# Gated linear unit: the tanh kept in its PSUM bank, two gates in one slot, the product taken for the hi and the lo part

## The chip, the cores and the metric

One core of one Trainium2 chip. Engines: TensorE (PE in the rows), VectorE (DVE), ScalarE (ACT), GpSimd (POOL) and SyncE (SP), which issues the DMAs. The metric is the device time of one execution in microseconds (us); the kernel before takes 1267.82 us, the median of three runs that lie between 1267.17 and 1268.06.

## The reference

A two-layer decoder trunk on x[1024, 1024] in float32. Each layer normalises x, projects it to queries, keys, values, an SSM input and three gates, runs three groups side by side, and projects their gated outputs back into the residual:

```python
h = _rms(x, norm_g[l])
z = h @ w_in[l]
aq, ak, av, ag, su, sg, xq, xg = split(z)
out_a = sliding_window_attn(aq, ak, av, sinks[l]) * silu(ag)
out_b = s5(su, ...) * silu(sg)
out_c = cross_attn(xq, mk, mv) * silu(xg)
x = x + concat([out_a, out_b, out_c]) @ w_out[l]
```

The edited code is the end of s5, the SSM group, which is 512 channels wide, together with the gate that follows it:

```python
y = gelu(y)
y = y * sigmoid(y @ w_glu + b_glu)
out_b = y * silu(sg)
```

With sigmoid(v) = (1 + tanh(v/2))/2 the output is (1 + tanh(v/2)) * y * silu(sg)/2. The halves are folded into weights and stored gates, so that the kernel computes (tanh + 1) * g * y.

## The kernel before, in words

Float32 matmuls are made of three passes over operands that are split into a hi and a lo part of a rounded format (names in h and l: yh and yl, wh and wl, gh and gl). Their sum is the float32 value, and a float32 tensor that feeds a matmul is split by a ScalarE cast (hi) and a GpSimd or VectorE subtraction (lo).

Every operation is recorded on a tape first. A list scheduler (`order`, line 210) then lays the whole tape out with a cost for each instruction (`price`, line 349), and `issue` (line 323) emits it; so each engine's instructions stand in an order that is fixed when the kernel is built, and all carry line 333 in the profile. Engines run their own order and wait for one another by semaphores. SBUF is cut into slots by a table (`PLAN`, line 59): a name may lie in the slots listed for it, and a slot's next tile waits for the last user of the one before. PSUM is dealt out by the scheduler itself, in eight banks, at most two of them at a time for tiles of kind kq (`CAP`, line 344); a tile takes the bank that has been free the longest and holds it until its last user is done.

The unit `glu` (line 1391) is woven with the cross-attention into the memory (names xq, xpr, xph, xpl, bg, xg) in `run`, at line 1568, and the scheduler fills TensorE from what comes next too: the output projection of the attention group (mm, gh, gl, o, mg) and, in layer 1 of the input, the last columns of the gate projections (fc, fg), which are stored to gscr in DRAM. For each of two halves of the sequence the unit loads y from yscr, splits it into yh and yl, and makes four blocks m of 128 channels. A block takes twelve matmuls of 128x512 into a kq tile, a gate g fetched from gscr by a DMA, the elementwise work, and `mixed_store` (line 784), which splits the result into the hi and lo tiles o of the output projection (a ScalarE cast and a GpSimd subtraction). There are 2 layers, 2 halves and 4 blocks: 16 gates in all.

The gate's SBUF home is `gt`, slot R0 alone (line 92), 128x1024 wide. Before, it holds one gate at a time: g in one half, the tanh in the other. So block m+1 can fetch its g only when the o of block m are made. The kq bank is read once, by the tanh.

Of the kernel before, what the change touches and what calls it, by code (L numbers as in the profile page):

```python
# [11 lines left out]
F32 = mybir.dt.float32  # L12
F32R = mybir.dt.float32r
I32 = mybir.dt.int32
AF = mybir.ActivationFunctionType
ALU = mybir.AluOpType
# [383 lines left out]
class Trunk:  # L400
# [990 lines left out]
    def glu(self, l):  # L1391
        nc, a = self.nc, self.a
        bg = self.t("bglu", [P, 4])
        b0 = self.t("yt", [P, 512])[0:4, 0:P]
        nc.sync.dma_start(b0, a["b_glu"][l].rearrange("(m p) -> m p", p=P))
        pb = self.bg1()
        nc.tensor.transpose(pb[:, 0:4], b0, self.ident[0:4, 0:4])
        nc.scalar.activation(bg, pb[:, 0:4], AF.Copy, scale=0.5)
        wv = a["w_glu"][l].rearrange("(k p) n -> p k n", p=P)
        ws = [self.wload([(None, wv[:, :, 256 * i : 256 * i + 256])], [P, 4, 256], 0.5, "m") for i in range(2)]  # L1400
        for half in range(2):
            yp = [[self.t(n, [P, 2, 512], F32R) for _ in range(2)] for n in ("yh", "yl")]
            yh, yl = ([z[m // 2][:, m % 2] for m in range(4)] for z in yp)
            for m in range(4):
                yt = self.t("yt", [P, 512])
                jh = slice(half * 64, half * 64 + 64)
                nc.sync.dma_start(yt.rearrange("p (s j) -> p s j", s=LC), self.ys[m][:, :, jh])

                ov = lambda z: z.rearrange("p (b s j) -> p b s j", b=4, s=LC)
                yv = yt.rearrange("p (s b j) -> p b s j", s=LC, b=4)  # L1410
                nc.scalar.copy(ov(yh[m]), yv)
                nc.gpsimd.tensor_tensor(ov(yl[m]), yv, ov(yh[m]).bitcast(F32), op=ALU.subtract)
                yield
            self.mixed(1, half)
            for m in range(4):
                wh, wl = ws[m // 2]
                c = slice(m % 2 * P, m % 2 * P + P)
                ps = self.mm1("kq")
                n = 0
                for k in range(4):  # L1420
                    for w, y in ((wh, yh), (wh, yl), (wl, yh)):
                        nc.tensor.matmul(ps, w[:, k, c], y[k], start=n == 0, stop=n == 11)
                        n += 1
                th, g = self.carve("gt", [512, 512])
                nc.sync.dma_start(g, self.gscr[1, half, m])
                nc.scalar.activation(th, ps, AF.Tanh, bias=bg[:, m : m + 1])
                nc.vector.scalar_tensor_tensor(th, th, 1.0, g, op0=ALU.add, op1=ALU.mult)
                nc.gpsimd.tensor_tensor(g, yh[m].bitcast(F32), yl[m].bitcast(F32), op=ALU.add)
                nc.vector.tensor_tensor(g, g, th, op=ALU.mult)
                self.mixed_store(1, half, m, g)  # L1430
                yield

# [181 lines left out]
```

## Time and profile before

| | us |
|---|---|
| median of three runs | 1267.82 |
| profiled execution | 1271.33 |
| its span in the trace | 1269.6 |
| TensorE busy | 1237.5 (97%) |
| VectorE busy | 843.1 (66%) |
| ScalarE busy | 544.9 (43%) |
| GpSimd busy | 363.7 (29%) |
| mean granted TensorE clock | 0.995 of full speed |

The trace is of one execution. An engine that is 97% busy leaves some 32 us of idle time; the rows below show where in the edited stretches that idle time lies, and what ended it: an arrow "<-DVE xg" behind an idle time says that VectorE's instruction writing xg was the last thing waited for. Idle time of the other engines costs nothing in itself.

### The profile page before, as it was taken

How to read it: one execution, taken by the hardware profiler on the slowest of the kernel's cores; microseconds unless marked ns; L12 is line 12 of the kernel's file. 1: busy time of each engine (PE TensorE's matmuls, PEld its weight loads, DVE VectorE, ACT ScalarE, POOL GpSimd, SP SyncE). 2: the span in 40 equal slices, each digit the busy share in tenths (PEclk: the TensorE clock that was granted, in tenths of full speed). 3: DMA queues.
4: the chain of work that ended last, by engine and by line, in shares of the span. 5: the costliest groups of instructions: out<-in, count | busy, mean ns of one | idle time of the engine just before them, and what ended most of it. 6: DMA issues, size and time to landing. Idle time of an engine off the chain costs nothing.

```text
span 1269.6 us, 20347 instructions
## 1 busy us (share of the span) xinstructions
PE 1237.5 (97%) x7179; PEld 1046.1 (82%) x7179; DVE 843.1 (66%) x1941; ACT 544.9 (43%) x1320; POOL 363.7 (29%) x585
## 2 busy tenths in 40 slices
PE   8999999999999999899999999999999999899998
PEld 6987888898887988688878787899797897668886
DVE  6879889747788678632477888865787675444311
ACT  5463323336566666310344223344656575442100
POOL 1371010154342366310082100044342211283100
PEclk9999999999999999999999999999999999999999
DMA  8254545511225765773554555441313542377532
GB/s 245 62 138 114 150 138 170 145 45 54 85 77 153 212 184 150 214 224 125 183 136 114 145 145 147 120 113 42 105 35 124 174 131 76 98 235 244 177 108 75
DMA packets 190456, 171.79 MB, mean 135 GB/s; under 512 B 59625, under 2 KB 142097, under 8 KB 190354
## 3 DMA queue, kind: packets, MB, share of 16 engines
q1 hardware_dynamic: 190354, 170.48, 46.0%
q8 instruction: 57, 0.93, 0.3%
q14 instruction: 45, 0.37, 0.1%
HBM read 114.81 MB, written 46.72 MB: 127 GB/s over the span
## 4 chain that ended last, share of the span: by engine, by line
PE 82%; DMA 7%; DVE 4%; ACT 3%; POOL 2%; issue 2%; SPq 1%; DVEq 0%; ACTq 0%; POOLq 0%
PE mm L333 27%; PE fc L333 23%; PE bg L333 17%; PE kq L333 13%; DMA so<-kscr 3%; PE tp L333 2%; POOL o L333 1%; DMA raw<-in_w_in 1%; DMA x<-xr 1%; DMA xt<-x 1%; DMA graw<-in_w_out 1%; DMA gt<-gscr 1%; DMA gscr<-fg 1%; DVE hl L333 1%; SPq L333 1%
## 5 line engine op out<-in xcount | busy, mean ns | idle before, releaser
L333 PE MATMUL fc<-hh,fh 128*128 128x512 f32 x512 | 205.2, 401 | 2.0 <-DVE fg L333 1.6
L333 PE MATMUL fc<-hl,fh 128*128 128x512 f32 x512 | 205.7, 402 | 0.0
L333 PE MATMUL fc<-hh,fl 128*128 128x512 f32 x512 | 204.2, 399 | 0.1
L333 PE MATMUL mm<-ph,o 128*128 128x512 f32 x512 | 161.4, 395 | 0.0
L333 PEld LDWEIGHTS fc<-hh,fh 128*128 128x128 f32 x512 | 96.4, 188 | 21.7 <-DVE fg L333 2.4
L333 PEld LDWEIGHTS mm<-ph,o 128*128 128x128 f32 x512 | 95.9, 188 | 21.7
L333 PEld LDWEIGHTS fc<-hh,fl 128*128 128x128 f32 x512 | 96.7, 189 | 19.5 <-issue 1.2
L333 PEld LDWEIGHTS fc<-hl,fh 128*128 128x128 f32 x512 | 96.7, 189 | 17.1
L333 PE MATMUL kq<-ml,hh 128*128 128x256 f32 x384 | 109.2, 285 | 0.0
L333 PE MATMUL kq<-mh,hh 128*128 128x256 f32 x384 | 108.7, 286 | 0.0
L333 PE MATMUL kq<-mh,hl 128*128 128x256 f32 x384 | 108.7, 284 | 0.0
L333 PE MATMUL mm<-pl,o 128*128 128x512 f32 x256 | 101.1, 395 | 0.0
L333 PE MATMUL mm<-gh,o 128*128 128x512 f32 x256 | 85.4, 402 | 7.3 <-ACT gh L333 3.6
L333 POOL COPY ifs<-f 128x16 f32<-128x16 f32 x64 | 18.8, 315 | 209.8 <-PE tp L333 209.0
L333 DVE TENSOR_TENSOR xr<-xr,mm 128x512 f32<-128x512 f32 x32 | 21.9, 685 | 85.6 <-PE mm L333 85.5
L333 PEld LDWEIGHTS kq<-ml,hh 128*128 128x128 f32 x384 | 72.9, 190 | 1.4 <-issue 0.8
L333 PEld LDWEIGHTS kq<-mh,hh 128*128 128x128 f32 x384 | 72.7, 190 | 1.2 <-ACT aph L333 0.4
L333 PEld LDWEIGHTS kq<-mh,hl 128*128 128x128 f32 x384 | 72.7, 189 | 0.2
L333 ACT ACTIVATE apr<-apr,anm 128x256 f32<-128x256 f32 (+1 forms) x128 | 61.7, 484 | 19.9 <-DVE anm L333 19.8
L333 PEld LDWEIGHTS mm<-gh,o 128*128 128x128 f32 x256 | 48.7, 191 | 20.7 <-ACT gh L333 4.0
L333 PE MATMUL mm<-hl,wh 128*128 128x256 f32 (+1 forms) x192 | 62.8, 329 | 1.0 <-DVE hl L333 1.0
L333 PE MATMUL mm<-hh,wh 128*128 128x256 f32 (+1 forms) x192 | 60.8, 327 | 1.4 <-ACT wh L333 1.1
(259 smaller groups left out, 3001.0 us busy)
## 6 DMA issues: line engine op xcount, KB each, us to landing
fraw<-in_w_in SPq DMA_DIRECT2D x32, 512.0 KB
gscr<-fg SPq DMA_DIRECT2D x48, 256.0 KB
kraw<-in_w_mem_kv SPq DMA_DIRECT2D x16, 512.0 KB
xm<-mg SPq DMA_DIRECT2D x32, 256.0 KB
xr<-xm SPq DMA_DIRECT2D x32, 256.0 KB
praw<-in_w_out SPq DMA_DIRECT2D x16, 512.0 KB
mraw<-in_w_in SPq DMA_DIRECT2D x12, 512.0 KB
xt<-in_x SPq DMA_DIRECT2D x8, 512.0 KB
```

What stands on the lines that cost most here:

```text
L333: ins = op.fn(*map(self.real, op.a), **{k: self.real(x) for k, x in op.kw.items()}).ins
```

## The change

For each pair of blocks one gt tile is made, and each of its halves holds the g of one block. The tanh is written back into its own PSUM bank. VectorE forms g = (tanh + 1) * g, reading the bank, and then writes g * yh into the bank; GpSimd multiplies g by yl in place; VectorE adds the bank to it. GpSimd's former sum yh + yl is gone. The bank's last user is therefore the add, not the tanh.

```diff
@@ -1421,12 +1421,16 @@
                     for w, y in ((wh, yh), (wh, yl), (wl, yh)):
                         nc.tensor.matmul(ps, w[:, k, c], y[k], start=n == 0, stop=n == 11)
                         n += 1
-                th, g = self.carve("gt", [512, 512])
+
+                if m % 2 == 0:
+                    gs = self.carve("gt", [512, 512])
+                g = gs[m % 2]
                 nc.sync.dma_start(g, self.gscr[1, half, m])
-                nc.scalar.activation(th, ps, AF.Tanh, bias=bg[:, m : m + 1])
-                nc.vector.scalar_tensor_tensor(th, th, 1.0, g, op0=ALU.add, op1=ALU.mult)
-                nc.gpsimd.tensor_tensor(g, yh[m].bitcast(F32), yl[m].bitcast(F32), op=ALU.add)
-                nc.vector.tensor_tensor(g, g, th, op=ALU.mult)
+                nc.scalar.activation(ps, ps, AF.Tanh, bias=bg[:, m : m + 1])
+                nc.vector.scalar_tensor_tensor(g, ps, 1.0, g, op0=ALU.add, op1=ALU.mult)
+                nc.vector.tensor_tensor(ps, g, yh[m].bitcast(F32), op=ALU.mult)
+                nc.gpsimd.tensor_tensor(g, g, yl[m].bitcast(F32), op=ALU.mult)
+                nc.vector.tensor_tensor(g, g, ps, op=ALU.add)
                 self.mixed_store(1, half, m, g)
                 yield
 
```

Since costs and users of tiles change, the scheduler lays out the surroundings of the unit anew. On TensorE in layer 0, second half of the unit, before: two kq tiles (kq_5762 and kq_5929) end, transposes into bg follow, and the next kq tile begins in a bank that was not theirs.

```text
kq: result of the unit's matmuls; bg: cross-attention; mm: output projection; fc: input projection
```

```order
L333 MATMUL kq_5762<-yl_5963,mh_5274 128x512
L333 MATMUL kq_5762<-yh_5935,ml_5301 128x512
L333 MATMUL kq_5929<-yl_5963,mh_5274 128x512
L333 MATMUL kq_5929<-yh_5935,ml_5301 128x512
L333 MATMUL bg_6036<-ident_65,xpr_5833 128x128 x2
L333 MATMUL bg_6046<-ident_65,xpr_5833 128x128 x2
L333 MATMUL bg_6049<-xpl_6058,xvh_5175 128x512
L333 MATMUL kq_6071<-yh_5711,mh_5397 128x512
L333 MATMUL kq_6071<-yl_5720,mh_5397 128x512
L333 MATMUL kq_6071<-yh_5711,ml_5412 128x512
```

After, the same place, on TensorE. kq_5754 and kq_5768 end with the four kq matmuls just above these rows; kq_6068 takes the bank of kq_5754.

```order
L333 MATMUL bg_6028<-ident_65,xpr_5817 128x128 x4
L333 MATMUL bg_6036<-ident_65,xpr_5817 128x128 x4
L333 MATMUL mm_5996<-gh_5228,o_993_5106 128x512
L333 MATMUL mm_5996<-gh_5228,o_992_5067 128x512
L333 MATMUL mm_5996<-gl_5247,o_992_5067 128x512
L333 MATMUL mm_5996<-gh_5228,o_993_5106 128x512
L333 MATMUL bg_6055<-xph_6049,xvh_5175 128x512
L333 MATMUL bg_6060<-ident_65,xpr_5858 128x128
L333 MATMUL bg_6062<-ident_65,xpr_5858 128x128
L333 MATMUL bg_6060<-ident_65,xpr_5858 128x128
L333 MATMUL bg_6062<-ident_65,xpr_5858 128x128
L333 MATMUL kq_6068<-yh_5681,mh_5397 128x512
```

Two transposes groups, four mm and one bg matmul lie between the two tiles of the same bank.

On TensorE in layer 1, first half, before: the last matmuls of kq_11421 and kq_11490 are followed by four scores (bg from xkh and xkl) and by kq_11684, which takes kq_11421's bank.

```order
L333 MATMUL kq_11490<-yl_11584,mh_11383 128x512
L333 MATMUL kq_11490<-yh_11578,ml_11398 128x512
L333 MATMUL bg_11677<-xkh_11114,xq_11637 128x256
L333 MATMUL bg_11677<-xkl_11126,xq_11637 128x256
L333 MATMUL bg_11677<-xkh_11114,xq_11637 128x256 x2
L333 MATMUL kq_11684<-yh_11405,mh_11470 128x512
L333 MATMUL kq_11684<-yl_11415,mh_11470 128x512
L333 MATMUL kq_11684<-yh_11405,ml_11485 128x512
```

After, at the same place, from the last of the scores on: kq_11717 takes the bank of kq_11425, whose last matmul stands seven matmul rows above these.

```order
L333 MATMUL bg_11682<-xkh_11118,xq_11642 128x256
L333 MATMUL fc_11530<-hh_1088_6744,fl_10762 128x512
L333 MATMUL fc_11700<-hh_1127_6942,fh_10745 128x512
L333 MATMUL fc_11700<-hl_1129_6952,fh_10745 128x512
L333 MATMUL fc_11700<-hh_1127_6942,fl_10762 128x512
L333 MATMUL fc_11700<-hh_1127_6942,fh_10745 128x512
L333 MATMUL fc_11700<-hl_1129_6952,fh_10745 128x512
L333 MATMUL fc_11700<-hh_1127_6942,fl_10762 128x512
L333 MATMUL fc_11700<-hh_1127_6942,fh_10745 128x512
L333 MATMUL fc_11700<-hl_1129_6952,fh_10745 128x512
L333 MATMUL fc_11700<-hh_1127_6942,fl_10762 128x512
L333 MATMUL kq_11717<-yh_11409,mh_11474 128x512
```

Ten fc matmuls moved in front of the third kq tile; a fourth, kq_11739, follows right behind it, where before the fourth came 186 rows later.

On VectorE in layer 1, between the two halves, before: the weights' lo part gl, the two instructions of one gate (gt), products for the cross-attention (xg) and the projection (mg), the next gl, the next gate.

```order
L333 TENSOR_TENSOR gl_12133<-graw_12022,gh_12120 128x1024
L333 SCALAR_TENSOR_TENSOR gt_12125<-gt_12125 128x512
L333 TENSOR_TENSOR gt_12125<-gt_12125 128x512
L333 TENSOR_TENSOR xg_1932_12138<-xg_1932_12138,bg_11596 128x512
L333 TENSOR_TENSOR mg_12102<-mg_12102,mm_12129 128x512
L333 TENSOR_TENSOR xg_1941_12151<-xg_1941_12151,bg_11635 128x512
L333 TENSOR_TENSOR gl_12211<-graw_12145,gh_12192 128x1024
L333 SCALAR_TENSOR_TENSOR gt_12205<-gt_12205 128x512
L333 TENSOR_TENSOR xg_1979_12219<-xg_1979_12219,bg_11825 128x512
L333 TENSOR_TENSOR gt_12205<-gt_12205 128x512
```

After, at the same place: both gates of a pair stand together, behind two xg, an mg and a gl; kq_11717 is the bank that the next kq tile, kq_12266, takes.

```order
L333 TENSOR_TENSOR xg_1928_12172<-xg_1928_12172,bg_11601 128x512
L333 TENSOR_TENSOR xg_1937_12177<-xg_1937_12177,bg_11640 128x512
L333 TENSOR_TENSOR mg_12134<-mg_12134,mm_12164 128x512
L333 TENSOR_TENSOR gl_12220<-graw_12174,gh_12202 128x1024
L333 SCALAR_TENSOR_TENSOR gt_12182<-kq_11717,gt_12182 128x512
L333 TENSOR_TENSOR kq_11717<-gt_12182,yh_11583 128x512
L333 SCALAR_TENSOR_TENSOR gt_12182<-kq_11739,gt_12182 128x512
L333 TENSOR_TENSOR kq_11739<-gt_12182,yh_11583 128x512
L333 TENSOR_TENSOR gt_12182<-gt_12182,kq_11717 128x512
L333 TENSOR_TENSOR xg_1973_12212<-xg_1973_12212,bg_11878 128x512
L333 TENSOR_TENSOR gt_12182<-gt_12182,kq_11739 128x512
```

The two gates moved behind xg, xg, mg and gl, and the add that frees the bank of kq_11717 is the ninth row.

## Rows read from the trace of the kernel before

**Rows 1.** Page, part 1: engine, busy us, share of the span, instructions.

```profile
PE 1237.5 (97%) x7179; PEld 1046.1 (82%) x7179; DVE 843.1 (66%) x1941; ACT 544.9 (43%) x1320; POOL 363.7 (29%) x585
```

**Rows 2.** Page, part 4: the chain that ended last, by engine.

```profile
PE 82%; DMA 7%; DVE 4%; ACT 3%; POOL 2%; issue 2%; SPq 1%; DVEq 0%; ACTq 0%; POOLq 0%
```

**Rows 3.** Timeline of TensorE, layer 0: start, us, engine, instruction, count, idle before and its releaser.

```profile
525.50 0.97 PE L333 MATMUL mm<-gh,o 128*128 128x512 f32 x3 [3.59 <-ACT gh L333]
```

**Rows 4.** Timeline of TensorE, layer 1.

```profile
1060.22 0.39 PE L333 MATMUL bg<-xkh,xq 128*128 128x256 f32 x1 [0.75 <-ACT xpr L333]
...
1108.81 0.50 PE L333 MATMUL mm<-gh,o 128*128 128x512 f32 x1 [1.88 <-DVE fg L333]
...
1122.09 0.74 PE L333 MATMUL mm<-gh,o 128*128 128x512 f32 x2 [0.21 <-POOL o L333]
...
1125.73 0.50 PE L333 MATMUL mm<-gh,o 128*128 128x512 f32 x1 [0.34 <-DVE xg L333]
...
1130.04 0.50 PE L333 MATMUL mm<-gh,o 128*128 128x512 f32 x1 [1.25 <-DVE xg L333]
...
1137.53 0.73 PE L333 MATMUL kq<-yh,mh 128*128 128x512 f32 x2 [0.16 <-ACT yh L333]
...
1141.74 0.50 PE L333 MATMUL kq<-yl,mh 128*128 128x512 f32 x1 [0.71 <-POOL yl L333]
```

**Rows 5.** Chain that ended last, in order of time, four stretches: start, us, what, count.

```profile
492.61 2.87 DMA gt<-gscr
...
525.45 0.04 issue
...
1119.09 4.92 DMA gt<-gscr
...
1156.62 2.78 PE kq L333 x12
1159.40 104.39 PE mm L333 x451
```

**Rows 6.** Busy time by stretch: us, then busy us (count) per engine, clock, DMA share, GB/s.

```profile
520.00:560.00 40.00, 36.41 (x152) 29.15 (x151) 18.82 (x23) 9.62 (x14) 9.14 (x10) 0.96 0.73 229
...
1100.00:1120.00 20.00, 18.05 (x73) 13.97 (x72) 8.17 (x9) 10.11 (x17) 12.98 (x10) 0.91 0.64 205
1120.00:1140.00 20.00, 18.04 (x75) 13.21 (x74) 10.24 (x11) 8.73 (x18) 19.23 (x17) 1.00 0.77 244
```

**Rows 7.** Tile gt: engine, operation, count: ns min/median/max, first and last start, forms.

```profile
L333 ACT ACTIVATE gt<-kq,bglu x16: 682/688/692, 466.2 to 1176.1; 128x512 f32<-128x512 f32 x16
L333 DVE SCALAR_TENSOR_TENSOR gt<-gt x16: 684/692/1761, 466.9 to 1184.4; 128x512 f32<-128x512 f32 x16
L333 POOL TENSOR_TENSOR gt<-yh,yl x16: 1276/1304/2224, 467.8 to 1185.2; 128x512 f32<-128x512 f32 x16
L333 DVE TENSOR_TENSOR gt<-gt x16: 680/691/1776, 469.6 to 1186.5; 128x512 f32<-128x512 f32 x16
```

**Rows 8.** Groups by shape: engine, operation, shapes, count, busy us, mean ns, idle before.

```profile
L333 DVE SCALAR_TENSOR_TENSOR fg<-fg,fc 128x512 f32<-128x512 f32 x48 | 32.8, 684 | 19.1 <-ACT fg L333 18.7
...
L333 ACT ACTIVATE fg<-fc 128x512 f32<-128x512 f32 x48 | 28.4, 592 | 34.3 <-PE fc L333 32.2 <-issue 1.1 <-ACT wht L333 0.9
```

**Rows 9.** Timeline of VectorE, both layers.

```profile
516.16 1.27 DVE L333 TENSOR_TENSOR xg<-xg,bg 128x512 f32<-128x512 f32 x2
...
1117.82 0.69 DVE L333 TENSOR_TENSOR xg<-xg,bg 128x512 f32<-128x512 f32 x1 [0.56 <-DMA xg<-gscr]
1118.42 1.22 DVE L333 TENSOR_TENSOR gl<-graw,gh 128x1024 fp32r<-128x1024 f32 x1
1124.10 0.98 DVE L333 SCALAR_TENSOR_TENSOR gt<-gt 128x512 f32<-128x512 f32 x1 [4.46 <-DMA gt<-gscr]
```

**Rows 10.** Timeline of ScalarE, layer 1.

```profile
1117.15 1.05 ACT L333 CAST gh<-graw 128x1024 fp32r<-128x1024 f32 x1 [1.82 <-DMA graw<-in_w_out]
```

**Rows 11.** Timeline of GpSimd, layer 1.

```profile
1120.76 2.53 POOL L333 TENSOR_TENSOR o<-mg,o 128x512 fp32r<-128x512 f32 x2
```

## The prediction

> **What bounds the kernel now.** I read the page's busy row first, then the chain, then TensorE's waits, then the two places where the edited code runs. TensorE is busy 1237.50 of 1269.6 us [rows 1], and the chain that ended last lies on it for 82% [rows 2]. So a VectorE, ScalarE or GpSimd instruction costs time only where TensorE waits for what it makes; the time after is the time before plus what TensorE's idle gaps and its slow-clock stretches gain or lose. The profiled execution took 1271.33 us, 1.7 more than its span, and lies 3.5 above the median of 1267.82; I form differences in the trace and add them to the median.
>
> The gated linear unit runs twice, about 442 to 561 us (layer 0) and 1050 to 1191 us (layer 1). There TensorE's gaps are few. Layer 0: 3.59 us for the weight cast gh [rows 3]. Layer 1: 0.75 at 1060.22, 1.88 at 1108.81, then 0.21, 0.34, 1.25, 0.16 and 0.71 up to 1141.74 [rows 4]; these last five sum to 2.67, and the unit is followed by 104 us of output matmuls in one unbroken piece [rows 5], so nothing lost in the unit is won back later. [...]
>
> **The change, part by part.** Counts first. ScalarE keeps its 16 tanh, now PSUM to PSUM. VectorE's two instructions per gate become three: 16 more of 0.69 us, 11 us on an engine busy 66% of the span [rows 1, 7]. GpSimd keeps 16 operations of 1.30 us [rows 7]: the sum yh+yl becomes the product g*yl. DMAs, matmuls and casts keep their numbers. By count alone this costs nothing, because none of it is on TensorE.
>
> What a VectorE instruction costs with a PSUM operand is seen in the gate of the input projection, fg<-fg,fc: 684 ns over 48 [rows 8]. Those of the linear unit, SBUF to SBUF, take 692 and 691 at the median, up to 1761 and 1776 at the longest [rows 7]. The trace has no VectorE instruction of this size that writes PSUM and no tanh that does. For these I take 0.69 us each, the value of the nearest rows. The bounds: the shortest pass of this size in these rows is ScalarE's fg<-fc at 592 ns [rows 8], the longest VectorE's 1776; nothing excludes either, so a chain of tanh, two VectorE products and an add ranges from 0.4 us shorter to about 4 longer than I take it. It matters only at the places (b) to (d) below.
>
> [...]
>
> What does cost is that the PSUM bank is held longer. Before, a kq bank was free after the tanh: 0.69 us behind the last matmul. Now it is free after tanh 0.69, gate 0.69, product 0.69, GpSimd's product 1.30 (it overwrites g, so it waits for VectorE's) and the add 0.69: 4.06, with a hop of 0.04 us from each engine to the next (as between the cast gh and TensorE at 525.45 [rows 5]) some 4.3 us. Only two banks may hold kq tiles, and in the new order the next tile of the same bank waits for that add. TensorE runs in order, so everything behind that kq matmul waits too. Where the order puts less than 4.3 us of matmuls between the end of one tile and the first matmul of the next in its bank, TensorE stands still. I walked the order with 0.23 us per matmul of 512 columns (twelve in 2.78 [rows 5]) and half of that for 256:
>
> (a) Layer 0, first half and first handover of the second: 5.6 and 8.8 us lie between. No stall.
> (b) Layer 0, kq_6068 after kq_5754: two kq matmuls, eight transposes, five projection matmuls and four transposes, about 3.0 us, against 4.3 us. Stall 1.4 (0 to 2.5).
> (c) Layer 1, kq_11717 after kq_11425: two kq matmuls, six scores, ten fc matmuls, about 3.5 us, against 4.8, because VectorE has an fg instruction and both gates of the pair ahead of the first add. Stall 1.35. The 0.75 wait at 1060.22 [rows 4] is for a softmax that now has 24 more matmuls in front of it, and goes. Net +0.6 (-0.7 to +2).
> (d) Layer 1, kq_12266 after kq_11717, the largest. Behind the wait for fg (1108.81) stand 42 matmuls, 9.7 us, 11.3 with the dip: TensorE is at kq_12266 at 1120.2. The add it needs stands in VectorE's order behind two xg products, an mg and a gl, then two gates and two products. In the old trace the second xg starts at 1117.82, held by its DMA, and gl at 1118.42 for 1.22 [rows 9], held by its weights, whose cast starts at 1117.15 [rows 10]. The gate pair is fetched once GpSimd's o<-gt of the former pair frees the slot, about 1112, and a fetch takes 4.92 us at this place (from 1119.09) and 2.87 at another (from 492.61) [rows 5]: it is there by 1115 to 1117 and not last. An mg of 0.69 now stands between xg and gl, so VectorE is free at 1117.82 + 0.69 + 0.69 + 1.22 = 1120.4; the first product ends at 1121.8, the second at 1123.2. GpSimd has the first of two o<-mg in front until about 1122.0 (1120.76 plus half of 2.53 [rows 11]) and ends its product at 1123.4; the add ends at 1124.1, or 3.9 after TensorE's arrival. I take 3.6, since twelve kq matmuls more stand ahead in (c) than before, and TensorE may reach all of this a little later. Stall 3.6 (1.5 to 6). What stood late there before comes along: of the 2.67 us of gaps I let 1.2 stand, because they are for the same xg, o and yl. Net +2.1 (-1.5 to +4).
> (e) The weights graw of layer 0, whose cast ended the 3.59 gap [rows 3]. Their buffer is freed by a gl that VectorE now does behind xg, mg and xg, three times 0.64 to 0.69 (two xg took 1.27 [rows 9]): 2.0 us later. TensorE has 34 matmuls in front of the place instead of 24, 2.3 us. -0.3 (-2 to +2.5).
> (f) A gap of 3.6 at (d) is of the size that was followed by a dip (1.88 and 3.59), and the two dips of today stay: +1.6 (0 to +3.2).
>
> [...]
>
> Sum: 1.4 + 0.6 + 2.1 - 0.3 + 1.6 = +5.4 on the median, 1273.2 us.
>
> **Rivals.** *The pair slot pulls the unit forward (faster).* Two gates are now loaded for one freeing of the slot. Before, the single slot made VectorE wait 4.46 us for gt at 1124.10 [rows 9], and each later gate came behind it. Should the pair's gates and the second xg be in by about 1116, the add of (d) is done before 1120.2 and nothing stands still; then the 0.75 and the 2.67 go, and if (e) comes out at -2 with (b) small the sum is -5.4: 1262.4. For it: the fetch of the pair is issued some 7 us earlier than 1119.09. Against: xg and gl stand in front of it on VectorE, and they were late for reasons that the change leaves as they are.
>
> *Nothing that can be measured.* Within 0.2% of the median, 2.5 us, is what a measurement of this kernel can't tell from no change. TensorE's waits would be moved rather than added: kq stalls, and then xg, o and yl, which came later than kq, are in time. Full compensation: (d) net 0, (b) hidden, no new dip: +0.1, 1267.9. For it: 2.67 us of gaps right behind (d) are there to absorb it. Against: (b) and (c) have no gap behind them.
>
> *Every handover stalls (slower still).* If VectorE's instructions run beside GpSimd's at their longest, 1.76 [rows 7], for two of its three instructions, each chain is 2 us longer; the handovers of (b), (c) and (d) each lose 2 more and one more dip follows: +5.4 + 6 + 1.6, 1280.8. The slowed ones before had SBUF operands only, of which the product and the gate now have a PSUM one; so this is the less likely.
>
> **How the numbers follow.** The stalls forecast rest on a walk through the order with old times, and two of them are differences of about 1 us between figures of 3 to 5; the gaps that they may eat are as large. Slower as summed 0.42, slower still 0.10, no change 0.21, faster 0.27. The likeliest is the sum, 1273.2, its own range 1270 to 1277. The range with the other cases: 1262 to 1279. Faster by over 0.2% 0.27, within 0.21, slower 0.52.
>
> **What would show it.** (b), (c), (d): gaps of TensorE ahead of a kq matmul, ended by VectorE's gt, at about 525, 1058 and 1120 us; before, no kq matmul waited for VectorE. (e): the gap for gh near 525 of 3 to 3.6. (f): granted clock below 1.00 in a second window between 1100 and 1140. Wrong, if TensorE has no gap ahead of kq, or if the gaps between 1120 and 1142 fall to under 0.5 in sum without a new one: then the pair slot decides. Wrong in its prices, if the tanh, gate or product with PSUM operands is far from 0.69.

## The result, and the profile after

The changed kernel takes 1278.62 us (median of four, 1275.62 to 1282.22), the kernel before 1267.49 on the same chip: a ratio of 1.0094, 95% interval 1.0074 to 1.0114. It is 11.1 us slower where 5.4 were forecast. The profiled execution took 1279.56 us with a span of 1277.8, which is 8.2 above the span before; the medians are 11.1 apart, because the profiled execution of before lies 3.8 above its median and that of after 0.9. What is read from the two traces is rough by the difference, some 3 us. The busy row of the page of after, against [rows 1]:

```profile
PE 1239.1 (97%) x7179; PEld 1046.8 (82%) x7179; DVE 854.1 (67%) x1957; ACT 543.9 (43%) x1320; POOL 362.1 (28%) x585
```

TensorE's work is the same; VectorE has the 16 instructions and 11.0 us more that were counted. What each costs is in the tile views of after, for kq and gt (ns min/median/max), against [rows 7]:

```profile
L333 ACT ACTIVATE kq<-kq,bglu x16: 653/662/681, 463.9 to 1157.7; 128x512 f32<-128x512 f32 x16
...
L333 DVE SCALAR_TENSOR_TENSOR gt<-kq,gt x16: 676/683/691, 464.8 to 1164.1; 128x512 f32<-128x512 f32 x16
L333 DVE TENSOR_TENSOR kq<-gt,yh x16: 699/716/1795, 465.6 to 1164.8; 128x512 f32<-128x512 f32 x16
L333 POOL TENSOR_TENSOR gt<-gt,yl x16: 1265/1296/1314, 466.4 to 1166.3; 128x512 f32<-128x512 f32 x16
L333 DVE TENSOR_TENSOR gt<-gt,kq x16: 672/673/689, 468.7 to 1168.6; 128x512 f32<-128x512 f32 x16
```

All medians are within 30 ns of the 0.69 and 1.30 us that the forecast took. So it isn't the price of an instruction. Where the time went stands in TensorE's gaps. First layer 0 of after (start, us, instruction, idle before and what ended it), against the one gap of [rows 3]:

```profile
469.64 1.17 PE L333 MATMUL bg<-ones,xpr 128*128 128x2 f32 x8 [1.19 <-ACT xpr L333]
...
511.36 0.70 PE L333 MATMUL bg<-ident,xpr 128*128 128x128 f32 x4 [0.90 <-DVE xpr L333]
512.22 0.50 PE L333 MATMUL kq<-yh,mh 128*128 128x512 f32 x1 [0.16 <-DVE gt L333]
...
529.40 1.20 PE L333 MATMUL mm<-gh,o 128*128 128x512 f32 x4 [2.83 <-ACT gh L333]
532.85 0.79 PE L333 MATMUL mm<-gl,o 128*128 128x512 f32 x1 [2.24 <-DVE gl L333]
```

The wait for the weights, 3.59 before, is 2.83 for the cast gh and 2.24 for its low part gl. Layer 1 of after, the same view, against [rows 4]:

```profile
1060.08 0.50 PE L333 MATMUL fc<-hh,fh 128*128 128x512 f32 x1 [1.41 <-DVE fg L333]
...
1077.77 0.61 PE L333 MATMUL fc<-hh,fh 128*128 128x512 f32 x1 [1.07 <-DVE fg L333]
...
1107.69 0.50 PE L333 MATMUL fc<-hh,fh 128*128 128x512 f32 x1 [0.97 <-DVE fg L333]
...
1116.93 0.50 PE L333 MATMUL mm<-gh,o 128*128 128x512 f32 x1 [0.70 <-DVE fg L333]
...
1121.58 1.22 PE L333 MATMUL mm<-gh,o 128*128 128x512 f32 x2 [3.91 <-POOL o L333]
...
1131.13 0.72 PE L333 MATMUL mm<-gh,o 128*128 128x512 f32 x2 [0.42 <-POOL o L333]
...
1134.28 0.50 PE L333 MATMUL kq<-yh,mh 128*128 128x512 f32 x1 [0.57 <-DVE gt L333]
```

A wait for fg is a wait for a PSUM bank of the input projection: VectorE's fg is the last to read an fc tile, and the next fc or mm tile takes its bank. Such waits are not new. Before had 0.52, 0.41, 0.73 and 1.88 of them between 1070 and 1109, 3.54 in sum; after has the four shown and one of 0.40 at 1092.45, 4.55 in sum.

The largest gap, 3.91, is in front of an output matmul and not of a kq one. Its cause is read from GpSimd's timeline there:

```profile
1114.33 1.28 POOL L333 TENSOR_TENSOR o<-gt,o 128x512 fp32r<-128x512 f32 x1 [1.77 <-PE fc L333]
1115.58 2.52 POOL L333 TENSOR_TENSOR o<-xg,o 128x512 fp32r<-128x512 f32 x2
1118.06 2.24 POOL L333 TENSOR_TENSOR o<-gt,o 128x512 fp32r<-128x512 f32 x1
1120.27 1.26 POOL L333 TENSOR_TENSOR o<-mg,o 128x512 fp32r<-128x512 f32 x1
```

The first o<-gt waits for the last fc matmul, because these o tiles lie in the buffers of hh and hl, which fc reads. The operand o<-mg for which TensorE stands still is the fifth instruction of this list; before it was the fourth, without the second o<-gt. Before, twelve kq matmuls stood in TensorE's order at this place, and no gap followed them. In the new order they were done some 210 matmuls earlier, so TensorE arrives with nothing to do.

The granted clock by stretch (us, busy us and count, clock, DMA share, GB/s), on TensorE alone, against [rows 6]:

```profile
520.00:560.00 40.00, 34.93 (x139) 0.91 0.75 236
...
1100.00:1120.00 20.00, 15.82 (x72) 0.97 0.38 120
1120.00:1140.00 20.00, 17.42 (x65) 0.86 0.73 250
```

520 to 560 falls from 0.96 to 0.91 and 1120 to 1140 from 1.00 to 0.86, while 1100 to 1120 rises from 0.91 to 0.97; 440 to 480, with the gap of 1.19, falls from 1.00 to 0.96. More time at the lower level, 0.50 of the full clock, stands behind the gaps: in slices of 1 us it fills those from 527 to 529 and from 1111 to 1113 in before, and from 532 to 538 and from 1119 to 1125 in after. In an unbroken row a 128x512 matmul starts every 0.43 us there and every 0.23 elsewhere. Summed over the trace, gaps above 0.15 us ahead of a matmul go from 4.66 to 8.53 us between 430 and 650, from 7.87 to 11.41 between 1020 and 1178, and fall by 1.0 elsewhere; matmuls in slow stretches lose some 4.0 us before and 7.5 after against the same shapes outside, worked out from their start times. 6.4 + 3.5 = 9.9 of a difference of 8.2 in the spans; the rest, -1.7, is spread thinly over other matmuls.

### The profile page after: what moved, and what is told of

The parts are those of the page before. It is cut to its first block, busy times and chain, and to the rows that moved or that the text cites. A ratio compares the mean times of both kernels' runs of the same rounds, so it can differ in the third digit from the quotient of the medians.

```text
span 1277.8 us, 20362 instructions
## 1 busy us (share of the span) xinstructions
PE 1239.1 (97%) x7179; PEld 1046.8 (82%) x7179; DVE 854.1 (67%) x1957; ACT 543.9 (43%) x1320; POOL 362.1 (28%) x585
## 4 chain that ended last, share of the span: by engine, by line
PE 84%; DMA 5%; DVE 5%; ACT 2%; issue 1%; POOL 1%; SPq 0%; ACTq 0%; POOLq 0%; DVEq 0%
PE mm L333 29%; PE fc L333 24%; PE bg L333 16%; PE kq L333 13%; DMA so<-kscr 2%; PE tp L333 2%; DMA yt<-yscr 1%; DMA xpr<-gscr 1%; ACT xpr L333 1%; DVE hl L333 1%; DVE gt L333 1%; DVE fl L333 0%; DMA praw<-in_w_out 0%; POOL o L333 0%; DVE kq L333 0%
```

## The experiments

In them each engine's order is that of before or of after, held by a list, or the scheduler's own for that kernel. The operations of a gate are emitted in one form or another, and in a list single instructions can be moved. A list holds the order of the instructions but not the PSUM banks: these are dealt out anew, and up to three kq tiles may hold a bank at a time instead of two. The kq banks of the unit are those of after in s1, s2, s4 and s24 and those of before in b1, b4 and b14; in e1, e2, e6, s24e and s24t some differ, so that a difference there can come from the banks too. s1, the list of after with one move, has the ratio of after, so the list by itself costs nothing that shows.

All ratios are to the kernel before, run on the same chip (its median was 1266.66, 1267.58, 1267.48 and 1265.50 in the four sets), so kernels of different sets are compared by ratio; 0.001 is 1.27 us. The ratio is taken over all executions and is not the quotient of the two medians, from which it differs by up to 0.0014 (s24t: 1268.00 over 1265.50 is 1.0020). Where a quoted expectation names a theory by a letter: O, the new order costs and not the new work; H, the bank held over the chain costs; F, the two-gate slot moves cover away; W, the longer work per gate costs.

| kernel | order | work per gate | us | ratio [95%] |
|---|---|---|---|---|
| e1 | before | as changed | 1281.50 | 1.0127 [1.0106, 1.0148] |
| e6 | before | as changed, bank freed early | 1272.13 | 1.0037 [1.0023, 1.0052] |
| e2 | after | as changed, bank freed early | 1276.90 | 1.0090 [1.0068, 1.0111] |
| e3 | own | as changed, bank freed early | 1278.13 | 1.0098 [1.0079, 1.0118] |
| e4 | own | as changed, one gate to a slot | 1271.64 | 1.0051 [1.0033, 1.0069] |
| e5 | own | two gates to a slot, two VectorE operations | 1271.60 | 1.0035 [1.0015, 1.0054] |
| p1 | nudged | as before | 1268.74 | 1.0016 [1.0005, 1.0027] |
| s1 | after, one move | as changed | 1277.82 | 1.0094 [1.0077, 1.0111] |
| s2 | after, layer 0 moved | as changed | 1274.40 | 1.0062 [1.0046, 1.0078] |
| s4 | after, layer 1 moved | as changed | 1276.13 | 1.0073 [1.0053, 1.0094] |
| s24 | after, both moved | as changed | 1272.46 | 1.0043 [1.0025, 1.0061] |
| s24e | as s24 | bank freed early | 1269.86 | 1.0044 [1.0029, 1.0058] |
| s24t | as s24 | as e5 | 1268.00 | 1.0034 [1.0019, 1.0049] |
| b1 | before, layer 0 moved | as before | 1266.84 | 0.9997 [0.9976, 1.0018] |
| b4 | before, layer 1 moved | as before | 1270.15 | 1.0044 [1.0030, 1.0057] |
| b14 | before, both moved | as before | 1269.98 | 1.0049 [1.0031, 1.0066] |

### Work or order: e1, e2, e6

e1 emits the new operations in the old order; e2 and e6 keep the product in the SBUF slot, so that the bank is free after the gate, in the order of after (e2) and of before (e6):

```diff
-nc.vector.tensor_tensor(ps, g, yhm, op=ALU.mult)
+nc.vector.tensor_tensor(g, g, yhm, op=ALU.mult)
 nc.gpsimd.tensor_tensor(g, g, ylm, op=ALU.mult)
-nc.vector.tensor_tensor(g, g, ps, op=ALU.add)
+nc.vector.tensor_tensor(g, g, g, op=ALU.add)
```

> The changed arithmetic and the pair slot, but every engine's instructions in the order of the kernel before (each gate's product placed right behind its first VectorE instruction). Theory O (the loss comes from the new order, not from the work): 1265 to 1270 us, the 3.91 us gap for o at 1121 and the 5.1 us of gaps for gh and gl near 530 are gone, three or four stretches at the lower clock. Theory B (the loss comes from the bank that is held 4.3 us and the third VectorE instruction): 1274 us or more, with gaps of TensorE ahead of kq matmuls or of what VectorE does behind the gates.

> The order of the changed kernel, the same five instructions per gate on the same engines, but the product stays in SBUF (g*yh, then times yl, then doubled, so the output differs): the bank is free after the first VectorE instruction, 1.4 us behind the matmuls instead of 4.3. Theory O: 1275 to 1281, as the changed kernel; only the two gaps ahead of kq matmuls (0.16 and 0.57 us) go. Theory B: 1270 or less.

> The pair slot and three VectorE instructions per gate in the order of the kernel before, but with the bank free after the first of them (product kept in SBUF, output differs). The run with the held bank in this order took 1281.5 us, with a 5.65 us gap ahead of a kq matmul. Theory H (in the old order it is the held bank that costs, the pair slot and the third instruction nothing): 1265 to 1270, the 5.65 gap gone. Theory P (the pair slot and the third instruction cost in the old order): 1276 or more.

In the old order the new work costs 15 us, more than in its own, where theory O had expected 1265 to 1270. TensorE's timeline of e1:

```profile
1113.95 0.79 PE L343 MATMUL kq<-yh,mh 128*128 128x512 f32 x1 [5.65 <-DVE gt L343]
...
1131.55 0.76 PE L343 MATMUL mm<-gh,o 128*128 128x512 f32 x1 [4.70 <-DVE xg L343]
```

This is the stall that term (d) forecast, for kq and ended by VectorE's gt, but in an order that the change doesn't have. With the bank freed early (e6) 1.48 of it are left, and an output matmul waits 3.94 for gt. TensorE's timeline of e6:

```profile
1106.51 0.79 PE L343 MATMUL kq<-yh,mh 128*128 128x512 f32 x1 [1.48 <-DVE gt L343]
...
1122.17 0.47 PE L343 MATMUL mm<-gh,o 128*128 128x512 f32 x1 [3.94 <-DVE gt L343]
```

So at the order of before the held bank is worth 1.0127 - 1.0037 = 0.0090, 11 us. The 0.0037 that remain, 4.7 us, are more than theory H allowed (1272.13 against 1265 to 1270). At the order of after (e2) the held bank is worth 0.0004, nothing that can be measured, though the gaps ended by gt and the 1.41 for fg do go. So the held bank is not what costs in the new order. What is left there is the order itself, and with it, not separated in this order, the slot and the third VectorE operation.

### Which part makes the order: e3, e4, e5, p1

e3 is e2's arithmetic, planned anew. e4 keeps the three VectorE operations and the bank, with a slot per gate. e5 keeps the two-gate slot and the bank, with the arithmetic of before:

```diff
 nc.scalar.activation(ps, ps, AF.Tanh, bias=bg[:, m : m + 1])
-nc.vector.scalar_tensor_tensor(g, ps, 1.0, g, op0=ALU.add, op1=ALU.mult)
-nc.vector.tensor_tensor(ps, g, yhm, op=ALU.mult)
-nc.gpsimd.tensor_tensor(g, g, ylm, op=ALU.mult)
-nc.vector.tensor_tensor(g, g, ps, op=ALU.add)
+nc.vector.scalar_tensor_tensor(ps, ps, 1.0, g, op0=ALU.add, op1=ALU.mult)
+nc.gpsimd.tensor_tensor(g, yhm, ylm, op=ALU.add)
+nc.vector.tensor_tensor(g, g, ps, op=ALU.mult)
```

p1 is the kernel before with the planner's cost of GpSimd's sum raised by 0.1 us, which moves some 80 instructions in the order and changes none.

> The same work as in the run with the freed bank, but laid out anew by the scheduler, which sees a bank that is free early and two gates per slot. If the pair slot alone leads the scheduler to a bad order: 1274 to 1282. If the held bank does: near 1268.

> The changed arithmetic (tanh and product in the bank, three VectorE instructions) with one gate per slot as before, laid out anew. If the held bank alone leads the scheduler to a bad order: 1274 to 1282. If the pair slot does: near 1268. If any new layout loses against a layout that was chosen, both this and the run before it lose.

> The pair slot and the tanh in its PSUM bank stay, but VectorE does two operations per gate as before (gate in the bank, then gate times the sum), GpSimd adds the hi and the lo part into the slot, and the list scheduler plans anew. The arithmetic of the sums differs from the change. Theory F (the pair slot lets the scheduler bring the gates' 12 kq matmuls forward, and the matmuls then lack as filler where fetches are late): the long gap near 1118 to 1122 that ends on an o cast or an xg fetch is still there, and the time is 1276 to 1280. Theory W (the third VectorE operation and GpSimd's product are what costs): 1271 or less.

> The kernel before, its arithmetic and slots untouched; only the scheduler is told that the GpSimd sum of a gate takes 0.1 us more, which changes the place of some 70 rows of the order around the unit. If any other layout of this place loses several us: 1271 or more. If the loss needs the change itself: within 2 us of before.

I had held the two-gate slot alone to blame; e5 speaks against that. Its long gap is there, and yet it is only 4.1 us above before. e5, at 1271.60, lies just above the range of theory W, and e4, at 1271.64, between its two cases. TensorE's timeline of e5:

```profile
1114.53 1.22 PE L343 MATMUL mm<-gh,o 128*128 128x512 f32 x2 [3.26 <-POOL o L343]
```

Its wait for gh in layer 0 is 2.10 and for gl 1.03. Neither the slot (e5) nor the longer chain (e4) gives the 1.0094; both together do, with the bank held (after) or not (e3). 0.0035 and 0.0051 add up to 0.0086, so the two may simply add. In all of these the order changes together with the work. The one new layout without new work costs little (p1), but it moves some 80 instructions where the change moves more than 400.

### The two late fetches: s1, s2, s4, s24

s1 moves GpSimd's o<-mg ahead of the two o<-xg and the second o<-gt. s2 (layer 0) moves the low parts gl ahead of an add and two gates on VectorE, and the fetch graw ahead of two praw, an xm and the gates' fetches on SyncE. s4 (layer 1) moves GpSimd's casts of xg and mg, which also free the xg buffers, and the fetches into these:

```diff
 GpSimd, layer 1 (s4)
+o201<-xg0, o201<-xg1, o001<-mg
 o101<-gt
-o201<-xg0, o201<-xg1
 o101<-gt
-o001<-mg
 SyncE, layer 1 (s4)
+xg0<-gscr
 gscr<-fg
+xg1<-gscr
 praw<-in_w_out
-xg0<-gscr
 graw<-in_w_out
-xg1<-gscr
```

> The changed kernel with one GpSimd instruction moved: layer 1, o<-mg ahead of two o<-xg and the second gate's o<-gt. Theory Q (GpSimd's queue sets the end of the 3.91 us gap at 1121.6): the gap falls below 1 us. If that gap was all that TensorE lost there: 1273 to 1275. Theory D (right behind it VectorE's add for kq_12266 binds, as it is late by itself): the gap ahead of kq grows from 0.57 to 3 or more and the time stays within 1.5 us of 1278.6.

> The changed kernel with three instructions moved, all in layer 0: the copy gl that frees the weights' buffer ahead of an add, an xpl, two xg and an mg; the fetch graw ahead of two praw, an xm and two gt; the next gl ahead of the last two gates. If the place of gl and graw in the queues is what makes the 2.83 and 2.24 us gaps near 530: both together fall from 5.1 to about 1, one or two stretches at the lower clock go with them, 1271 to 1275. If the weights' transfer is late for other reasons: within 1.5 us of 1278.6.

> The changed kernel, with its order kept but for layer 1: on GpSimd the two o<-xg and the o<-mg go ahead of the o<-gt, and on SyncE the two xg fetches go ahead of the gscr store and the praw fetch they stood behind. If the 3.91 us gap at 1121.6 is GpSimd's and SyncE's queue positions together (with the last fc matmul as the start), the xg fetch leaves about 2.4 us earlier, the gap falls to 1 to 1.5 in two pieces, and with the slow clock behind it the time is 1274 to 1276. If the matmuls that went forward are what lacks and nothing else can fill the place, some 3.5 us of gaps stay there and the time is 1277 to 1279.

> The changed kernel with both sets of moves: the weights of the output projection first in layer 0, and the xg fetches and casts first in layer 1. If the two losses are independent: 1278.6 less 4.2 (measured for layer 0) less 2.5 to 4 (layer 1), so 1270.4 to 1272, still above the kernel before by what the longer gate chain costs. If the gains don't add, because a fixed sum of waits moves on to the next late fetch: about 1274.

s1 gained nothing, against theory Q, and that told more than the view of GpSimd: the gap is as long, for another operand. TensorE's timeline of s1:

```profile
1121.40 0.80 PE L343 MATMUL bg<-xph,xvh 128*128 128x512 f32 x1 [3.92 <-DVE xg L343]
```

Behind the o<-mg came the xg product, whose fetch had been issued late. SyncE's timeline of after shows why, and that of s4, below it, what the move does:

```profile
1116.90 0.32 SPq L333 DMA_DIRECT2D gscr<-fg  x1
1117.57 0.38 SPq L333 DMA_DIRECT2D praw<-in_w_out  x1
1118.06 0.45 SPq L333 DMA_DIRECT2D xg<-gscr  x1
```

```profile
1113.23 0.32 SPq L343 DMA_DIRECT2D xg<-gscr  x1
1113.90 0.32 SPq L343 DMA_DIRECT2D gscr<-fg  x1
1114.47 0.32 SPq L343 DMA_DIRECT2D xg<-gscr  x1
```

With s4 the first fetch leaves 4.8 us earlier, at 1113.23 instead of 1118.06; 2.65 of that is the run's own lead at this place (the wait for fg of 1107.69 ends at 1105.04), so the move gives 2.2. The gap splits into 2.48 for o<-mg and 3.02 for a later cast of o; in the one trace the stretch 1020 to 1178 has as much idle time as after (11.69), the slow clock less of it (1.6 against 3.1), and the ratio falls by 0.0021, 2.7 us, which the intervals of the two kernels don't yet separate. s2 is clearer: the 2.83 and 2.24 of layer 0 become 0.24, a new 0.89 for xpl comes up, the slow stretch behind goes (a matmul every 0.23 us from 530.76 to 539), and the ratio falls by 0.0032, 4.1 us. Which of its three moves did it was not tried. With both, 0.0051 or 6.5 us are given back, about the sum. TensorE's timeline of s24, and its clock:

```profile
522.34 0.50 PE L343 MATMUL bg<-xpl,xvh 128*128 128x512 f32 x1 [0.89 <-DVE xpl L343]
...
531.29 1.20 PE L343 MATMUL mm<-gh,o 128*128 128x512 f32 x4 [0.35 <-ACT gh L343]
...
1114.26 0.74 PE L343 MATMUL mm<-gh,o 128*128 128x512 f32 x2 [0.68 <-POOL o L343]
...
1121.94 0.50 PE L343 MATMUL mm<-gh,o 128*128 128x512 f32 x1 [2.02 <-ACT o L343]
```

```profile
520.00:560.00 40.00, 38.52 (x165) 1.00 0.75 233
1100.00:1120.00 20.00, 17.39 (x76) 1.00 0.62 196
1120.00:1140.00 20.00, 16.81 (x70) 1.00 0.73 246
```

Both places keep the full clock. The same trace has 0.91 over 440 to 480, with a gap of 2.16 at 472 in which TensorE waits for a softmax (xpr); no move touches that one.

### What is left, and a control: s24e, s24t, b1, b4, b14

s24e and s24t put e2's and e5's arithmetic into the order of s24. b1 moves, in the kernel before, one praw fetch, its cast ph and pl behind graw, gh and gl; b4 has the moves of s4, b14 both.

> The changed kernel with both sets of moves, and the product kept in its SBUF slot, so that the PSUM bank is free behind the first of the three VectorE operations (the sum at the end then adds the lo product to itself, so the values differ). If the bank held over the chain makes the remaining 5 us: 1268 or less. If it makes what it made in the order of the change without the moves, 1.7: 1270.8.

> The changed kernel with both sets of moves, its order and its two-gate slot, but with two VectorE operations per gate (tanh and gate in the bank, then gate times the sum) and GpSimd's sum in place of its product. If the third VectorE operation makes the remaining 5 us: 1267 to 1269. If the order with the gates brought forward makes them: 1272, or a little above, as the bank is now held over GpSimd's sum too.

> The kernel before, with its order kept but for layer 0: the praw fetch, the ph cast and pl are put behind graw, gh and gl of the output projection. If the 3.59 us gap ahead of gh near 525.5 is a matter of queue positions alone, it falls to about 1, and the slow-clock stretch behind it may go: 1263 to 1266, below both kernels. If the fetch of graw is late for another reason (its slot, the DMA engines), the gap stays and the time is 1267 to 1268.

> The kernel before with the same moves in layer 1 that gave the changed kernel 2.5 us (o<-xg and one o<-mg ahead of o<-gt on GpSimd, the xg fetches ahead of the gscr store and the praw fetch on SyncE). If those 2.5 us were the change's loss (before has 12 kq matmuls behind the last fc, which cover the fetch), nothing moves: 1266.5 to 1268.5. If the positions are bad in any kernel: 1264.5 to 1265.5.

> The kernel before with both sets of moves, the weights first in layer 0 and the xg fetches first in layer 1. If the places bind the kernel before too: 1262 to 1265, which would beat both kernels. If the kernel before covers both, or gives the gain back at the next fetch, as the 7.33 us wait at 611 in the run with the layer 0 moves alone suggests: 1266 to 1268.

Against s24's 1.0043, freeing the bank gives 1.0044 and taking the third VectorE operation away 1.0034: neither is a difference that these intervals, some 0.0015 either way, can show. In us s24t lies at 1268.00, where I had expected the third operation to be shown; but before was at 1265.50 in that set, and by ratio it isn't. So what makes the 5 us left over is not shown. They need not lie in the new order: e6, in the order of before, has 1.0037.

Of the control: b1 takes the 3.59 wait of [rows 3] away, and the ratio, 0.9997, shows no gain. In its profiled execution, the slowest of twelve, TensorE waits later on for a residual row, where the kernel before waited 0.20:

```profile
611.04 1.09 PE L343 MATMUL bg<-ident,nh 128*128 128x128 f32 x4 [7.33 <-DVE nh L343]
```

So the weights' place is not worth 4 us in the kernel before as it is in after. b4 is no clean control: on GpSimd it puts the o<-gt that frees the old kernel's single gate slot three instructions back, and the tanh behind it holds the bank. TensorE and ScalarE of b4:

```profile
1107.24 0.80 PE L343 MATMUL kq<-yh,mh 128*128 128x512 f32 x1 [3.19 <-ACT gt L343]
```

```profile
1106.50 0.69 ACT L343 ACTIVATE gt<-kq,bglu 128x512 f32<-128x512 f32 x1 [3.02 <-POOL o L343]
```

Its 0.0044 is most likely the price of that and of the slower clock behind the wait (a matmul every 0.43 us instead of 0.23 from 1107.83 to 1110.82), and b14 has such a wait as well, of 2.92. Both missed their ranges. No version beat the kernel before beyond its interval.

## Why the prediction was wrong, point by point

The direction was right, the size half, 5.4 against 11.1. The step that failed is term (e), the weights of layer 0, put at -0.3: it followed them to the cast gh and left out their low part gl and the slower clock behind. Prices of instructions held. By terms:

(a) No stall at the first handovers: right.

(b) Layer 0, kq_6068, 1.4: 0.90 + 0.16 = 1.06 at 511 to 512. Nearly right in size, though most of it falls on the transposes in front, since their xpr stands behind the gate chain in VectorE's order; with two VectorE operations instead of three (s24t) the 0.90 is 0.16.

(c) 1.35 at 1058: 1.41 at 1060.08. That the numbers agree is luck, for the wait is another: the fc matmuls that the walk counted as cover for the kq bank stand still for a bank of their own, until ScalarE's fg and VectorE's fg have read it. The gate and the product in front of fg on VectorE don't make it: s24t has the same 1.41 without the product, and there VectorE is idle until ScalarE's fg is done. TensorE and VectorE of s24t:

```profile
1051.41 0.50 PE L343 MATMUL fc<-hh,fh 128*128 128x512 f32 x1 [1.41 <-DVE fg L343]
```

```profile
1050.66 0.69 DVE L343 SCALAR_TENSOR_TENSOR fg<-fg,fc 128x512 f32<-128x512 f32 x1 [0.64 <-ACT fg L343]
```

The 0.75 for the softmax went, as forecast. The walk's list of waits in layer 1 was short: it left out 0.52, 0.68, 0.41, 0.23 and 0.73 between 1070 and 1100, three of them for fg.

(d) 3.6 ahead of kq_12266 near 1120, less 1.47 of old gaps. The kq matmul waits 0.57, at 1134.28: the add ended at 1134.23 where the walk had 1124.1, but TensorE was there only at 1133.7 where the walk had 1120.2. In front of it are the 3.91 and 0.42 for o. So a gap of the forecast size came a few matmuls earlier, and from another cause. The walk counted the twelve kq matmuls that moved ahead as making TensorE a little later; it didn't see that they had been the cover for GpSimd's o and the xg fetch behind the last fc. That their absence is the cause is read from the order; no run put them back. e1 shows that the mechanism of (d) is real, 5.65, where the order leaves it.

(e) -0.3 for the weights of layer 0: this step failed most. 3.59 became 2.83 + 2.24, 1.5 more, and the clock of 520 to 560 fell to 0.91; s2 puts the whole at 4.1 us. The first half of the step came out near, partly by luck. "Their buffer is freed by a gl that VectorE now does behind xg, mg and xg" was right. That gl ended 4.8 us later, not 2.0, but TensorE also reached the place 4.7 us later (526.57 against 521.91), not 2.3, so the wait for gh fell by 0.76. VectorE and SyncE of before, then of after:

```profile
514.63 1.61 DVE L333 TENSOR_TENSOR gl<-graw,gh 128x1024 fp32r<-128x1024 f32 x1 [0.73 <-PE bg L333]
...
516.31 0.38 SPq L333 DMA_DIRECT2D graw<-in_w_out  x1
```

```profile
519.35 1.68 DVE L333 TENSOR_TENSOR gl<-graw,gh 128x1024 fp32r<-128x1024 f32 x1
...
519.72 0.86 SPq L333 DMA_DIRECT2D gt<-gscr  x2
521.06 0.38 SPq L333 DMA_DIRECT2D graw<-in_w_out  x1
```

In both kernels the fetch of graw leaves within 0.1 us of that gl's end, at 516.24 and 521.03. After, two praw, an xm and the two fetches of the gate pair stand ahead of it on SyncE, but they were issued by 520.58: the buffer came last, not the queue. What (e) put at nothing is the second half: the matmuls need the low part of these weights too. On VectorE five of the six instructions of a gate pair stand ahead of this next gl:

```profile
526.98 0.68 DVE L333 SCALAR_TENSOR_TENSOR gt<-kq,gt 128x512 f32<-128x512 f32 x1
...
530.28 0.67 DVE L333 TENSOR_TENSOR gt<-gt,kq 128x512 f32<-128x512 f32 x1
530.88 1.91 DVE L333 TENSOR_TENSOR gl<-graw,gh 128x1024 fp32r<-128x1024 f32 x1
```

The cast gh runs at 528.31, so without them gl could have run at 529.4, 1.5 us earlier.

(f) One dip more, 1.6: no run shows one price for a dip, as the forecast takes it here and, with 11.3 for 9.7, in (d). By the mean clock the two of [rows 6] lost 1.6 us (0.04 of 40) and 1.8 (0.09 of 20), those of after 3.6 over 520 to 560 (0.09 of 40) and 3.4 over 1100 to 1140 (0.03 and 0.14 of 20 each). In matmuls the slow stretches cost 3.5 us more, most of it in layer 0 (1.4 before, 4.4 after between 430 and 650), where none was forecast. About half of the increase lies in 440 to 480 and not behind the weights. And "the two dips of today" were three: before has 0.97 over 1050 to 1100 as well.

In the two traces layer 1 lost 3.5 + 0.5 = 4.0 us in gaps and clock, against 0.6 + 2.1 + 1.6 forecast there, near by luck, since the gaps are others; layer 0 lost 3.9 + 3.0 = 6.9, against 1.1. The rival of the pair pulled forward named what the scheduler does with it, but took it for a gain; "every handover stalls", whose 1280.8 is the nearest number, is e1 and not the change, where kq matmuls wait 0.16 and 0.57. The terms of the no-change rival add up to +0.3 and not to +0.1, which moves nothing else.

With a PSUM operand the instructions kept at the median the price that was taken: the gate with a PSUM source takes 683 ns, the product into PSUM 716, the add 673, the SBUF pair of before 692 and 691; the tanh takes 662 into PSUM against 688 into SBUF.

What stays open: the 5 us between s24 and the kernel before. Held bank and third operation were each tried and are below what can be measured in that order; the gaps for fg are only 1.0 us more in sum than before, and whether something spread thinly makes the rest, no run tells. Nor was the filler put back behind the last fc: the twelve kq matmuls read the first half's yh and yl, whose buffers the second half's casts take over before that place, so they can't be moved back alone, and it wasn't tried.

## What to carry to other kernels

When a list scheduler lays a changed kernel out anew, price what left a place as well as what came to it: matmuls that moved forward are cover that a late fetch or cast then lacks. For every wait that is already on TensorE, follow the fetch through to the end, what frees its buffer, what stands ahead of it on the issuing queue, and what stands ahead of its casts, because a queue position can be worth several us: three instructions moved gave back 4.1 us (s2), and five more 6.5 us in all (s24). The same place moved in the kernel before gave nothing (b1), so a wait that goes is not yet time won. A PSUM bank held over a chain of engines can cost nothing that shows in one order (e2) and 11 us in another (e1 against e6), so it is judged in an order and not by itself.

## What the runs showed of the hardware

VectorE's product into PSUM takes 716 ns at the median (699 to 1795); its two instructions with a PSUM source take 683 and 673. The granted clock of before and after has two levels, 1.00 and 0.50 of full speed. The length of a gap alone didn't tell how long the lower one stayed behind it. Over 520 to 560, 2.83 and 2.24 with four matmuls between them went with a mean clock of 0.91 (after), one gap of 3.59 with 0.96 (before). In s1, with 1.82 and 1.77 there, the four matmuls between them take 1.91 us instead of after's 1.20, and those behind start every 0.43 us up to 536.92; in b4, behind one gap of 2.62, they start every 0.23 from 522.92 on. s24 and s24t, without long gaps there, have 1.00. The same program varies by more than the changes in question: 1262.16 to 1272.57 over 26 executions of the kernel before in one set, so that a single profiled execution can't rank kernels 3 us apart.
